# Elementwise work at the start of a fused RWKV-7 and attention block: from POOL to DVE and ACT, the low-rank 1-mu columns formed from results, the first weights on ACT's queue, a second shift buffer

## The chip, the cores and the metric

The kernel runs on one core of a Trainium2 chip. The metric is device time in microseconds (us), the median of several executions. The engines are PE (TensorE, matrix products), DVE (VectorE), ACT (ScalarE), POOL (GpSimd) and SP (SyncE, which here only issues DMAs). PEld is PE's weight load, which overlaps PE. Each engine works through its instructions in a fixed order; the DMA queues of SP and ACT feed the same 16 DMA engines.

## The reference, cut to what matters

```python
def reference(x, ...):                       # x: (1, 256, 2048), D = 2048, branches of 1024
    h = _rms_norm(x, pre_norm_g)             # x * rsqrt(mean(x^2) + eps) * g
    proj = h @ w_in                          # 2048 -> 8 * 1024 + 2 * 2048
    p_r, p_k, p_v, z_r, q_a, k_a, v_a, z_a, m_r, m_a = split(proj)
    # RWKV branch
    r = p_r + (_shift(p_r) - p_r) * mu_rkv[0]     # k and v alike; _shift moves by one token
    dh = _shift(h) - h
    xw = h + dh * mu_wa[0]
    xa = h + dh * mu_wa[1]
    w = exp(-DECAY_SCALE * sigmoid(w0 + tanh(xw @ w1) @ w2))     # low-rank: 2048 -> 64 -> 1024
    a = sigmoid(a0 + (xa @ a1) @ a2)
    y = group_norm(recurrence(r, w, k, v, kk, a)) + bonus
    y_r = y * silu(z_r)
    y_a = _chunk_band_attention(q_a, k_a, v_a, rel_bias) * silu(z_a)
    u_r, u_a = y_r @ w_branch_rwkv, y_a @ w_branch_attn
    merged = sigmoid(m_r + b0) * u_r + sigmoid(m_a + b1) * u_a
    return x + _rms_norm(merged @ w_out, post_norm_g)
```

## The kernel before

All matrix products run at float32 precision in two parts: each operand is split into an upper part `wh` rounded to float32r and a lower part `wl`, and a product of 128 rows of weights (a k-tile) is three matmuls. A group of weights is four k-tiles by 256 columns (512 KB). For every group SP issues a load into one of three buffers `raw`, ACT makes `wh` (L82, a copy of 128x1024) and DVE makes `wl` (L83, `raw` minus `wh`); that pair of steps is the helper `split`. PE then runs the group (L277), first a `wh`, then a `wl`, and so on.

The function `run_plan` plays the list `plan`: the products k0 and r0 (the first 256 columns of k and r) group by group in turn, then v0, `lora` (the first layer of both low-rank paths), k2, r2, v2, k4 and so on, with q, k, v and z of the attention between them, the merge gates mr and ma, the branch outputs ur and ua, and last the output product o. The weights' parts are made two groups ahead of their use; a scheduler then fixes each engine's order, so the instructions of an engine wait in one line.

The products k0, r0, v0, lora and k2 run before the norm's factor is known. They use `hr`, which is x times the norm's weights and lacks the factor per token; such a product has 16 k-tiles and 96 matmuls. The tiles `hr_A` (k-tiles 0 to 7), `hr_yrl` and `hr_yrh` are made by `first_raw` (ACT L146 the upper part, DVE L147 the lower) from the tiles `xT_UV` and `xT_R`, which `first_raw` also loads (L140), together with the weights of k0 (L141). `second_raw` loads the weights of r0 (L156) and sums x squared into `xs`. The norm's factor comes from `norm_factor`: two additions (L344, L345), a product with ones on PE (`rb`), a square root on ACT and a reciprocal on DVE (L349) into `rones`. `normalise` (L351 to L363) then multiplies x by the factor on POOL (L356) and makes the normalised operand `hn` on ACT (L359) and DVE (L360); r2 is its first user.

The low-rank product takes 256 columns: 64 of w1 and 64 of a1, times 1 - mu, and the same 128 columns times mu, whose result is shifted by a token and added. `lora_weights` loads the 128 columns into a staging tile `wa` and makes the four groups `lab` on POOL: two multiplications by mu (L397) and one subtraction (L398) a group. `lora_raw` splits a group; `lora_done` multiplies the result by the norm's factor (L368), adds the shifted half (L411, L412) and applies tanh (L413). `lw` (L444) is the second layer's product.

The tile with tag `xs` holds a product's result times the norm's factor, for the shift by one token (`xsk`, `xsr`, `xsv`, L368, then the shifted multiply-add at L727; `lsh` in `lora_done`; also z of `project_zr`, L781). It has one buffer. At the very start PE runs nine products of ones (L125, `wp`), which nothing reads.

Of the kernel before, what the change touches and what calls it, by code (L numbers as in the profile page):

```python
# [17 lines left out]
# units of side work fed in per group of four weight tiles: of the fronts (while and after r, k, v are made), and  # L18
# of the chains and the attention, every BD groups
# [4 lines left out]
# buffers of weight tiles: as loaded, upper parts, lower parts  # L24
# [3 lines left out]
# the pair of the RWKV gates that waits in a place of its own  # L28
ZI = 6
# products of ones at the start  # L30
NWARM = 9
# how the first group is cut: first tile, number of tiles
FIRST = ((0, 2), (2, 2))
# order of the products between r, k, v and the merge: q (q and k), z (gate) of attention, v (its values, by 512
# columns), r (gate of the RWKV branch), each with the first of its two pairs of heads
# [13 lines left out]
# columns of the packed per-channel vectors  # L49
# [7 lines left out]
# column blocks of w_in  # L57
# [5 lines left out]
def kernel(ctx: ExitStack, tc, x, xt, vecs, w_in, wa1, w2, a2, w0, rel, w_br, w_ba, w_out, post_g, out):  # L63
# [14 lines left out]
    def col(t, o):  # L78
        return t[:, o:o + 1]
# [8 lines left out]
    def w_load(src, k0, c0, nm):  # L88
        """Rows of 4 tiles, 256 columns."""
        t = w_tile(nm)  # L90
        nc.sync.dma_start(t, src[k0 * P:(k0 + 4) * P, c0:c0 + 256].rearrange("(k p) c -> p k c", p=P))
        return t

    def wide_chunks(src, c0, nm):
        """Rows of 2 tiles, 512 columns."""
# [10 lines left out]
    # ---- x, channel-major: first times the norm's weights only, for the products that run before the norm's  # L106
    # factor is known, then normalised; each in two float32r parts that lie side by side ----
# [11 lines left out]
    # the tensor engine's clock rises after a few microseconds of work: products of ones, which nothing reads,  # L119
    # while the first tiles are loaded  # L120
# [13 lines left out]
    def first_raw(g):  # L134
        def f(wh, wl):
            xg = xT[g // 2][:, (g % 2) * 4:(g % 2) * 4 + 4, :]
            raw = raw8[:, 2 * g]
            for k, n in FIRST if g == 0 else ((0, 4),):
                rows = slice((4 * g + k) * P, (4 * g + k + n) * P)
                nc.sync.dma_start(xg[:, k:k + n, :], xt[rows, :].rearrange("(k p) t -> p k t", p=P))  # L140
                nc.sync.dma_start(raw[:, k:k + n, :], w_in[rows, O_K:O_K + 256].rearrange("(k p) c -> p k c", p=P))  # L141
# [47 lines left out]
    # sums inside a chunk of 64, counted from its middle: of the tokens before token n, n = 0..64  # L189
# [9 lines left out]
    # masks of the chunk matrices: before the token (first half), up to the token (second half)  # L199
# [6 lines left out]
    # blocks of 16 below the diagonal, inside the diagonal blocks of 32  # L206
# [12 lines left out]
    # derived vectors: 1-mu for r, k, v; halves of k_a, a0, the merge biases  # L219
# [824 lines left out]
```

## Time and profile before

| what | value |
|---|---|
| device time, three executions | 878.86, 879.15, 877.31 us; median 878.86 us |
| profiled execution: span from first to last instruction | 877.4 us |
| profiled execution's own device time | not recorded apart from the span; the median of the three executions lies 1.5 us above the span |
| mean granted TensorE clock | 0.994 of full speed |
| PE busy | 854.3 us, 97% of the span |
| DVE busy | 592.7 us, 68% |
| ACT busy | 445.9 us, 51% |
| POOL busy | 46.2 us, 5% |

The span runs from the first to the last instruction of one profiled execution; the device time holds a little before and after it. Busy shares are averages over stages with different limits: POOL's 46.2 us, for instance, lie nearly all in the first 55 us.

### The profile page before, as it was taken

The numbers are of one execution on the slowest core, as the hardware profiler recorded it, in microseconds if no ns is written. First come the engines' busy times: TensorE is split into PE (matmuls) and PEld (weight loads), VectorE is DVE, ScalarE is ACT, GpSimd is POOL, SyncE is SP. The second block draws the span as 40 slices with busy tenths as digits, with TensorE's granted clock in tenths as the row PEclk, the third lists the DMA queues.
The fourth block names the chain that finished last, engine by engine and source line by source line (L and its number), as shares of the span: only waits on it lengthen the run. The fifth ranks groups of instructions, "written<-read, shape, count | busy, mean of one in ns | idle before, by whom it ended". The sixth has DMA issues, their size and how long they took to land.

```text
span 877.4 us, 14844 instructions
## 1 busy us (share of the span) xinstructions
PE 854.3 (97%) x5972; PEld 730.7 (83%) x5972; DVE 592.7 (68%) x826; ACT 445.9 (51%) x669; POOL 46.2 (5%) x82
## 2 busy tenths in 40 slices
PE   8979999999899999999999999999999999999996
PEld 7978888888787888888888888888888888888886
DVE  7998886966759866654976775565565565565554
ACT  7466564545455433444556664445444455444442
POOL 4840000000010000000000000000000000000000
PEclk9999999999999999999999999999999999999999
DMA  9706545664144555634475446666556656676662
GB/s 305 210 19 187 172 123 150 198 171 130 50 121 141 172 149 146 194 115 145 129 222 154 144 144 205 183 189 191 182 182 189 190 184 182 187 264 213 194 193 96
DMA packets 142791, 147.33 MB, mean 168 GB/s; under 512 B 13313, under 2 KB 131201, under 8 KB 142338
## 3 DMA queue, kind: packets, MB, share of 16 engines
q1 hardware_dynamic: 130178, 138.96, 51.8%
q10 hardware_dynamic: 12544, 7.42, 2.8%
q8 instruction: 47, 0.77, 0.4%
q14 instruction: 22, 0.18, 0.1%
HBM read 143.74 MB, written 2.62 MB: 167 GB/s over the span
## 4 chain that ended last, share of the span: by engine, by line
PE 89%; DVE 4%; DMA 3%; SPq 2%; issue 1%; ACT 0%; DVEq 0%; ACTq 0%
PE acc_mr L277 10%; PE acc_ma L277 10%; PE acc_o L277 9%; PE acc_q L277 5%; PE acc_ak L277 5%; PE acc_va L277 5%; PE acc_ur L277 5%; PE acc_ua L277 5%; PE acc_za L277 5%; PE acc_k L277 4%; PE acc_v L277 4%; PE acc_r L277 4%; PE acc_zr L277 3%; DMA raw_v<-w_in_d 2%; PE pA L545 1%; PE acc_lora L277 1%
## 5 line engine op out<-in xcount | busy, mean ns | idle before, releaser
L277 PE MATMUL acc_mr<-hn,wh_mr 128*128 128x512 f32 x256 | 91.3, 400 | 0.0
L277 PE MATMUL acc_ma<-hn,wh_ma 128*128 128x512 f32 x256 | 91.1, 399 | 0.0
L277 PE MATMUL acc_mr<-hn,wl_mr 128*128 128x256 f32 x256 | 72.1, 282 | 0.0
L277 PE MATMUL acc_ma<-hn,wl_ma 128*128 128x256 f32 x256 | 72.0, 281 | 0.0
L83 DVE TENSOR_TENSOR wl_mr<-raw_mr,wh_mr 128x1024 fp32r<-128x1024 f32 x32 | 39.2, 1225 | 34.2 <-ACT wh_mr L82 34.1
L83 DVE TENSOR_TENSOR wl_o<-raw_o,wh_o 128x1024 fp32r<-128x1024 f32 x31 | 38.0, 1225 | 34.0 <-ACT wh_o L82 33.9
L83 DVE TENSOR_TENSOR wl_ma<-raw_ma,wh_ma 128x1024 fp32r<-128x1024 f32 x32 | 39.2, 1225 | 29.4 <-ACT wh_ma L82 29.4
L277 PEld LDWEIGHTS acc_mr<-hn,wh_mr 128*128 128x128 f32 x256 | 48.1, 188 | 12.4 <-issue 0.7
L277 PEld LDWEIGHTS acc_ma<-hn,wh_ma 128*128 128x128 f32 x256 | 48.1, 188 | 12.3 <-issue 0.6
L82 ACT ACTIVATE wh_ma<-raw_ma 128x1024 fp32r<-128x1024 f32 x32 | 33.9, 1060 | 45.0 <-PE acc_mr L277 37.3
L82 ACT ACTIVATE wh_mr<-raw_mr 128x1024 fp32r<-128x1024 f32 x32 | 34.0, 1061 | 39.3 <-PE acc_ua L277 16.2
L82 ACT ACTIVATE wh_o<-raw_o 128x1024 fp32r<-128x1024 f32 x31 | 32.8, 1059 | 39.6 <-PE acc_o L277 24.8
L277 PE MATMUL acc_o<-wh_o,mgh 128*128 128x512 f32 (+1 forms) x140 | 49.8, 356 | 0.0
L277 PE MATMUL acc_o<-wl_o,mgh 128*128 128x512 f32 (+1 forms) x140 | 49.8, 356 | 0.0
L277 PEld LDWEIGHTS acc_mr<-hn,wl_mr 128*128 128x128 f32 x256 | 48.4, 189 | 0.1
L277 PEld LDWEIGHTS acc_ma<-hn,wl_ma 128*128 128x128 f32 x256 | 48.3, 189 | 0.0
L277 PE MATMUL acc_q<-hn,wh_q 128*128 128x512 f32 x128 | 45.9, 398 | 0.0
L277 PE MATMUL acc_zr<-hn,wh_zr 128*128 128x512 f32 x128 | 45.9, 400 | 0.0
L277 PE MATMUL acc_za<-hn,wh_za 128*128 128x512 f32 x128 | 45.8, 399 | 0.0
L277 PE MATMUL acc_ak<-hn,wh_ak 128*128 128x512 f32 x128 | 45.8, 397 | 0.0
L277 PE MATMUL acc_va<-wh_va,hn 128*128 128x512 f32 x128 | 41.0, 395 | 0.0
L277 PE MATMUL acc_ak<-hn,wl_ak 128*128 128x256 f32 x128 | 36.8, 288 | 0.0
(478 smaller groups left out, 2385.1 us busy)
## 6 DMA issues: line engine op xcount, KB each, us to landing
raw_mr<-w_in_d SPq DMA_DIRECT2D x32, 512.0 KB, 4.2
raw_ma<-w_in_d SPq DMA_DIRECT2D x32, 512.0 KB, 3.6
raw_o<-w_out_d SPq DMA_DIRECT2D x32, 512.0 KB, 4.4
raw_v<-w_in_d SPq DMA_DIRECT2D x16, 512.0 KB, 4.7
raw_q<-w_in_d SPq DMA_DIRECT2D x16, 512.0 KB, 4.4
raw_ak<-w_in_d SPq DMA_DIRECT2D x16, 512.0 KB, 3.6
raw_zr<-w_in_d SPq DMA_DIRECT2D x16, 512.0 KB, 3.7
raw_va<-w_in_d SPq DMA_DIRECT2D x16, 512.0 KB, 3.8
```

The source lines that it names most:

```text
L82: ACT.activation(h, src, AF.Copy)
L83: DVE.tensor_tensor(l, src, h.bitcast(F32), op=ALU.subtract)
L277: PE.matmul(d, u, v, start=first and n == 0, stop=last and n == len(ops) - 1)
L545: PE.matmul(pA[h][:, c * P:(c + 1) * P], AB[HS[h], m, c, 2:4, :].rearrange("p a t -> p (a t)"), AB[HS[h], m, c, 0:2, :].rearrange("p a t - ...
```

## The change

Five edits; the diff also takes out comments, so line numbers behind `normalise` are lower by some lines after it.

1. `first_raw` issues the two loads of k0's first weight group on ACT's queue; the three later groups stay on SP's.
2. `normalise` no longer uses POOL. DVE multiplies x by the norm's weight and factor in one instruction a k-tile (16 of 128x256), in place; then `split` makes the two parts in four instructions of 128x1024 on ACT and four on DVE. Before, POOL made four products of 128x1024, ACT 16 and DVE 16 instructions of 128x256.
3. `lora_weights` has no staging tile: four loads of 256 KB go straight into the left halves of `lab` (before, two of 512 KB into `wa`). The eight multiplications by mu move to DVE, 256 elements a partition each. The columns times 1 - mu are no longer made (four POOL subtractions of 128x512 go); the left half stays unscaled, and `lora_done` subtracts the mu half of the result from it, one DVE instruction of 128x256 more.
4. The tiles with tag `xs` (also `lsh` and z) get two buffers.
5. The program's dynamic DMA scratch size is set to 1024.

```diff
-                nc.sync.dma_start(raw[:, k:k + n, :], w_in[rows, O_K:O_K + 256].rearrange("(k p) c -> p k c", p=P))
+                (nc.sync if g else nc.scalar).dma_start(raw[:, k:k + n, :], w_in[rows, O_K:O_K + 256].rearrange("(k p) c -> p k c", p=P))
...
-            POOL.tensor_tensor(xg, xg, rbc.unsqueeze(1).to_broadcast([P, 4, T]), op=ALU.mult)
             for i in range(4):
-                pre = col(vt, V_PRE + 4 * g + i)
-                ACT.activation(hg[:, i, 0, :], xg[:, i, :], AF.Copy, scale=pre)
-                DVE.scalar_tensor_tensor(hg[:, i, 1, :], xg[:, i, :], pre, hg[:, i, 0, :].bitcast(F32), op0=ALU.mult, op1=ALU.subtract)
+                DVE.scalar_tensor_tensor(xg[:, i, :], xg[:, i, :], col(vt, V_PRE + 4 * g + i), rbc, op0=ALU.mult, op1=ALU.mult)
+            split(hg[:, :, 0, :], hg[:, :, 1, :], xg)
             yield
...
         if not q:
-            lab.append(bg.tile([P, 16, 128], F32, tag="AB0", name="wa"))
             ab = bg.tile([P, 8, 256], F32, tag="AB1", name="lab0")
...
-        wa = lab[0][:, 8 * q:8 * q + 8]
-        nc.sync.dma_start(wa, wa1[q * 1024:(q + 1) * 1024, :].rearrange("(k p) c -> p k c", p=P))
         for g in (2 * q, 2 * q + 1):
-            w = lab[0][:, 4 * g:4 * g + 4]
-            ab = lab[1 + g]
+            nc.sync.dma_start(lab[g][:, :, 0:128], wa1[g * 512:(g + 1) * 512, :].rearrange("(k p) c -> p k c", p=P))
+
+    def lora_raw(g):
+        def f(wh, wl):
+            ab = lab[g]
             for n, o in ((0, V_MUW), (1, V_MUA)):
                 mu = vt[:, o + 4 * g:o + 4 * g + 4].unsqueeze(2).to_broadcast([P, 4, 64])
-                POOL.tensor_tensor(ab[:, :, 128 + 64 * n:192 + 64 * n], w[:, :, 64 * n:64 * n + 64], mu, op=ALU.mult)
-            POOL.tensor_tensor(ab[:, :, 0:128], w, ab[:, :, 128:256], op=ALU.subtract)
-
-    def lora_raw(g):
-        def f(wh, wl):
-            split(wh, wl, lab[1 + g])
+                DVE.tensor_tensor(ab[:, :, 128 + 64 * n:192 + 64 * n], ab[:, :, 64 * n:64 * n + 64], mu, op=ALU.mult)
+            split(wh, wl, ab)
...
-        sh = tp.tile([P, 2, T + 1], F32, tag="xs", name="lsh", bufs=1)
+        sh = tp.tile([P, 2, T + 1], F32, tag="xs", name="lsh", bufs=2)
...
-        DVE.tensor_tensor(t[0:64], sh[0:64, 0, 1:T + 1], sh[0:64, 1, 0:T], op=ALU.add)
-        DVE.tensor_tensor(za[64:128], sh[64:128, 0, 1:T + 1], sh[64:128, 1, 0:T], op=ALU.add)
+        DVE.tensor_tensor(t, sh[:, 0, 1:T + 1], sh[:, 1, 1:T + 1], op=ALU.subtract)
+        DVE.tensor_tensor(t[0:64], t[0:64], sh[0:64, 1, 0:T], op=ALU.add)
+        DVE.tensor_tensor(za[64:128], t[64:128], sh[64:128, 1, 0:T], op=ALU.add)
```

On ACT's queue the start of the program reads so before (`vt` are the packed vectors, `warm` is a first use of the square root, `wh_k` and `wh_r` the upper parts of the first weights, `xs` the sum of squares):

```order
L117 ACTIVATE warm<-warm 128x1
L1000 ACTIVATE warm<-warm 128x1
L146 ACTIVATE hr_A<-xT_UV,vt 128x256 x2
L82 ACTIVATE wh_k_163<-raw_77 128x512
L146 ACTIVATE hr_A<-xT_UV,vt 128x256 x2
L160 ACTIVATE xs_83<-xT_UV 128x1024
L82 ACTIVATE wh_k_163<-raw_77 128x512
L82 ACTIVATE wh_r_181<-raw_77 128x1024
```

and so after the change:

```order
L117 ACTIVATE warm<-warm 128x1
L141 DMA raw_77<-w_in_d 128x2x256 x2
L146 ACTIVATE hr_A<-xT_UV,vt 128x256 x4
L160 ACTIVATE xs_83<-xT_UV 128x1024
L995 ACTIVATE warm<-warm 128x1
L82 ACTIVATE wh_k_163<-raw_77 128x512
L82 ACTIVATE wh_r_181<-raw_77 128x1024
L82 ACTIVATE wh_k_163<-raw_77 128x512
```

The two DMA issues are new there, and the first `wh_k` has moved behind all four `hr_A` and the squares.

On DVE, around the low-rank product, before (`wl_lora` are the lower parts of its four groups, `xsk`, `xsr` and `xsv` the results of k0, r0 and v0 times the norm's factor, `k` and `r` their shifted sums):

```order
L83 TENSOR_TENSOR wl_lora_569<-lab_306,wh_lora_568 128x1024
L727 SCALAR_TENSOR_TENSOR k_494<-xsk_491,vt,k_494 128x256 x2
L360 SCALAR_TENSOR_TENSOR hn<-xT_UV,vt,hn 128x256 x2
L368 TENSOR_TENSOR xsr_499<-acc_r_234,rones 128x2x256
L83 TENSOR_TENSOR wl_lora_597<-lab_306,wh_lora_596 128x1024
L360 SCALAR_TENSOR_TENSOR hn<-xT_UV,vt,hn 128x256 x6
L727 SCALAR_TENSOR_TENSOR r_502<-xsr_499,vt,r_502 128x256 x2
L83 TENSOR_TENSOR wl_lora_632<-lab_Y,wh_lora_631 128x1024
L360 SCALAR_TENSOR_TENSOR hn<-xT_R,vt,hn 128x256 x2
L368 TENSOR_TENSOR xsv_624<-acc_v_513,rones 128x2x256
L360 SCALAR_TENSOR_TENSOR hn<-xT_R,vt,hn 128x256 x2
L83 TENSOR_TENSOR wl_lora_671<-lab_s,wh_lora_670 128x1024
```

and after, from the second group of `lora` on (before it now stand `xsk`, `xsr` and twelve of the new multiplications at L357):

```order
L357 SCALAR_TENSOR_TENSOR xT_R<-xT_R,vt,rones 128x256 x4
L83 TENSOR_TENSOR wl_lora_588<-lab_305,wh_lora_587 128x1024
L722 SCALAR_TENSOR_TENSOR k_483<-xsk_480,vt,k_483 128x256 x2
L722 SCALAR_TENSOR_TENSOR r_491<-xsr_488,vt,r_491 128x256 x2
L357 SCALAR_TENSOR_TENSOR xT_R<-xT_R,vt,rones 128x256
L83 TENSOR_TENSOR wl_lora_625<-lab_Y,wh_lora_624 128x1024
L357 SCALAR_TENSOR_TENSOR xT_R<-xT_R,vt,rones 128x256 x2
L83 TENSOR_TENSOR hn<-xT_UV,hn 128x4x256
L357 SCALAR_TENSOR_TENSOR xT_R<-xT_R,vt,rones 128x256
L83 TENSOR_TENSOR hn<-xT_UV,hn 128x4x256
L83 TENSOR_TENSOR wl_lora_663<-lab_s,wh_lora_662 128x1024
```

Behind it the line goes on with `hn`, `xsv` and the first `wl_k` of k2.

The third place is DVE in front of that, from the third group of k0 to the first group of `lora`, after the change (the multiplications by mu, L395, are new; the `wl` and `xs` rows stood there before too):

```order
L395 TENSOR_TENSOR lab_305<-lab_305,vt 128x4x64 x2
L83 TENSOR_TENSOR wl_k_260<-raw_77,wh_k_259 128x1024
L395 TENSOR_TENSOR lab_305<-lab_305,vt 128x4x64 x2
L83 TENSOR_TENSOR wl_r_298<-raw_77,wh_r_297 128x1024
L147 SCALAR_TENSOR_TENSOR hr_yrh<-xT_R,vt,hr_yrh 128x256 x4
L164 TENSOR_TENSOR xs_83<-xs_83,xsq_375 128x1024
L395 TENSOR_TENSOR lab_Y<-lab_Y,vt 128x4x64
L83 TENSOR_TENSOR wl_k_333<-raw_77,wh_k_332 128x1024
L395 TENSOR_TENSOR lab_Y<-lab_Y,vt 128x4x64
L83 TENSOR_TENSOR wl_r_371<-raw_77,wh_r_370 128x1024
```

Then follow `xs` 128x512, two `wl_v`, `xs` 128x256, the last two multiplications by mu, two more `wl_v`, the reciprocal and the first `wl_lora`.

## Rows read from the trace of the kernel before

**Rows 1.** The page's busy times, and the shares of the chain that ended last by engine.

```profile
PE 854.3 (97%) x5972; PEld 730.7 (83%) x5972; DVE 592.7 (68%) x826; ACT 445.9 (51%) x669; POOL 46.2 (5%) x82
PE 89%; DVE 4%; DMA 3%; SPq 2%; issue 1%; ACT 0%; DVEq 0%; ACTq 0%
```

**Rows 2.** The waits of PE over the whole run: who waits, for whom, us in all, how many, the longest.

```profile
PE acc_lora L277 <- DVE wl_lora L83: 4.7, 1, 4.7
PE acc_k L277 <- DVE wl_k L83: 2.7, 3, 1.8
PE pw L643 <- DVE SB L682: 1.3, 1, 1.3
PE lw L444 <- issue: 1.3, 1, 1.3
```

**Rows 3.** Four stretches of the run: the stretch, its length, then busy us (and instructions) of PE, PEld, DVE, ACT, POOL, then the granted clock, the DMA engines' busy share and GB/s.

```profile
26.50:34.00 7.50, 5.67 (x48) 5.47 (x47) 7.50 (x6) 3.05 (x3) 7.50 (x6) 1.00 0.66 146
46.00:54.00 8.00, 3.33 (x28) 3.13 (x27) 8.00 (x7) 3.70 (x9) 5.64 (x4) 1.00 0.00 0
54.00:58.00 4.00, 3.94 (x20) 3.94 (x21) 4.00 (x10) 4.00 (x8) 1.09 (x2) 0.57 0.02 6
82.00:877.40 795.40, 783.15 (x5455) 663.69 (x5454) 518.37 (x732) 392.01 (x583) 7.25 (x20) 1.00 0.54 167
```

**Rows 4.** POOL in order of time: start, busy us, the instructions, and in brackets the idle time before them and what ended it.

```profile
19.51 4.45 POOL L397 TENSOR_TENSOR lab<-wa,vt 128x256 f32<-128x256 f32 x4 [12.06 <-DMA wa<-wa_d]
...
34.69 2.27 POOL L398 TENSOR_TENSOR lab_s<-wa,lab_s 128x512 f32<-128x512 f32 x1
39.78 6.77 POOL L356 TENSOR_TENSOR xT_UV<-xT_UV,rones 128x1024 f32<-128x1024 f32 x2 [2.82 <-DVE rones L349]
46.51 5.09 POOL L356 TENSOR_TENSOR xT_R<-xT_R,rones 128x1024 f32<-128x1024 f32 x2
```

**Rows 5.** DVE in order of time, columns as in rows 4.

```profile
13.88 1.22 DVE L83 TENSOR_TENSOR wl_k<-raw,wh_k 128x1024 fp32r<-128x1024 f32 x1
...
18.87 1.22 DVE L83 TENSOR_TENSOR wl_k<-raw,wh_k 128x1024 fp32r<-128x1024 f32 x1
20.00 1.22 DVE L83 TENSOR_TENSOR wl_r<-raw,wh_r 128x1024 fp32r<-128x1024 f32 x1
...
26.41 2.29 DVE L83 TENSOR_TENSOR wl_k<-raw,wh_k 128x1024 fp32r<-128x1024 f32 x1
...
31.19 0.83 DVE L345 TENSOR_TENSOR xs<-xs 128x256 f32<-128x256 f32 x1
...
37.96 1.74 DVE L349 RECIPROCAL rones<-rones 128x256 f32<-128x256 f32 x1
39.70 1.23 DVE L83 TENSOR_TENSOR wl_v<-raw_v,wh_v 128x1024 fp32r<-128x1024 f32 x1
40.84 0.69 DVE L368 TENSOR_TENSOR xsk<-acc_k,rones 128x512 f32<-128x512 f32 x1
41.44 2.83 DVE L83 TENSOR_TENSOR wl_lora<-lab,wh_lora 128x1024 fp32r<-128x1024 f32 x1
44.20 5.19 DVE L727 SCALAR_TENSOR_TENSOR k<-xsk,vt,k 128x256 f32<-128x256 f32 x2
...
52.80 1.21 DVE L83 TENSOR_TENSOR wl_lora<-lab,wh_lora 128x1024 fp32r<-128x1024 f32 x1
53.93 2.46 DVE L360 SCALAR_TENSOR_TENSOR hn<-xT_UV,vt,hn 128x256 fp32r<-128x256 f32 x6
```

**Rows 6.** PE in order of time, at the two longest waits and at `lw`.

```profile
28.75 0.38 PE L277 MATMUL acc_k<-hr_yrh,wl_k 128*128 128x256 f32 x1 [1.83 <-DVE wl_k L83]
...
46.05 0.40 PE L277 MATMUL acc_lora<-hr_A,wh_lora 128*128 128x256 f32 x2
...
54.06 0.43 PE L277 MATMUL acc_lora<-hr_A,wl_lora 128*128 128x256 f32 x1 [4.73 <-DVE wl_lora L83]
54.29 0.63 PE L277 MATMUL acc_lora<-hr_A,wh_lora 128*128 128x256 f32 x2
...
57.93 0.40 PE L277 MATMUL acc_lora<-hr_A,wh_lora 128*128 128x256 f32 x2
...
58.29 0.40 PE L277 MATMUL acc_lora<-hr_yrl,wh_lora 128*128 128x256 f32 x2
...
72.27 1.95 PE L444 MATMUL lw<-w2e,zw 65*128 65x512 f32 x4 [1.27 <-issue]
```

**Rows 7.** The start on PE, ACT and SP's queue, in order of time.

```profile
5.57 0.79 PE L277 MATMUL acc_k<-hr_A,wh_k 128*128 128x256 f32 x2 [0.21 <-ACT wh_k L82]
14.65 0.50 PE L277 MATMUL acc_r<-hr_A,wh_r 128*128 128x256 f32 x2 [0.45 <-ACT wh_r L82]
...
0.81 0.45 ACTq L109 DMA_DIRECT2D vt<-vecs_d  x1
...
4.09 0.91 ACT L146 ACTIVATE hr_A<-xT_UV,vt 128x256 fp32r<-128x256 f32 x2 [1.07 <-DMA xT_UV<-xt_d]
...
10.04 1.71 ACT L146 ACTIVATE hr_A<-xT_UV,vt 128x256 fp32r<-128x256 f32 x4 [0.35 <-DMA xT_UV<-xt_d]
...
4.44 1.33 SPq L156 DMA_DIRECT2D raw<-w_in_d  x1
```

**Rows 8.** The DMA issued by SP between 33 and 36 us: transfer, count, KB each, median us from issue to landing.

```profile
raw_v<-w_in_d SPq DMA_DIRECT2D x1, 512.0 KB, 4.9
```

More of the change, by code (lines that the diff above doesn't have):

```diff
@@ L715, in done @@
             nmk = "rkv"[what]
-            xs = tp.tile([P, 2, T + 1], F32, tag="xs", name=f"xs{nmk}{j0}", bufs=1)
+            xs = tp.tile([P, 2, T + 1], F32, tag="xs", name=f"xs{nmk}{j0}", bufs=2)
             POOL.memset(xs[:, :, 0:1], 0.0)
@@ L780, in done @@
                 yrt.extend(bg.tile([P, n, 2, T], F32R, tag=t, name=f"yr_{t}") for t, n in (("AB1", 4), ("w2", 2), ("s", 2)))
-            z = tp.tile([P, 2, T], F32, tag="iv" if j0 == ZI else "xs", name=f"zr{j0}", bufs=1)
+            z = tp.tile([P, 2, T], F32, tag="iv" if j0 == ZI else "xs", name=f"zr{j0}", bufs=1 if j0 == ZI else 2)
             z_gate(acc, f"r{j0}", z)
@@ L1033 @@
     }
-    nc = bacc.Bacc("TRN2", target_bir_lowering=False, num_devices=1)
+    nc = bacc.Bacc("TRN2", target_bir_lowering=False, num_devices=1, dynamic_dma_scratch_size=1024)
     args, ins = [], {}
```

## The prediction

> **What bounds the kernel now.** I read the busy times first, then the chain, then PE's waits, and then the stretches in which PE waits. PE is busy in 97% of the span and holds 89% of the chain that ended last [rows 1], so time can only be won where PE idles or runs at a lower clock. Over the whole run its largest waits are 4.7 us in `lora` for a `wl_lora` of DVE, 2.7 us in three pieces for a `wl_k` of DVE, and 1.3 us before `lw` [rows 2]. After 82 us PE is busy 783.15 of 795.40 us and no wait that the list names is over 1.3 us [rows 2, 3]: the change must win its time before that.
>
> Two places carry the waits. At 28.75 us PE has waited 1.83 us for the last group of k0, and at 54.06 us 4.73 us for the second group of `lora` [rows 6]. In both stretches DVE and POOL are at work together: DVE is busy 7.50 of 7.50 us and 8.00 of 8.00, POOL 7.50 and 5.64 [rows 3]. The same instruction of DVE, a 128x1024 subtraction, took 1.22 us at 18.87 and at 20.00 us, before POOL began at 19.51 or just as it did, but 2.29 us at 26.41 and 2.83 us at 41.44 [rows 5], with POOL at work. POOL's first block ended at 34.69 + 2.27 = 36.96 us and its second began at 39.78 [rows 4]; in that gap the 1024 subtraction took 1.23 us again, at 39.70 us. Two shifted sums of 128x256 took 5.19 us at 44.20 us, 2.6 each; six instructions of that kind took 2.46 at 53.93, 0.41 each, when POOL had ended at 51.60 [rows 4, 5]. So DVE is slowed two to six times by POOL, and the late `wl` are what PE waits for.
>
> The Trainium skill, page "SBUF — State Buffer", section "SBUF: two separate sides", says why that may be: a DVE instruction with two SBUF operands and a GpSimd instruction that reads SBUF take one pair of ports in turn, and the one that comes later blocks until the other has ended. The traced 2.29 and 2.83 us against 1.22 agree with it. The sum below would be the same without the page.
>
> **The change part by part.** Prices of DVE alone, start to start: 128x1024 1.13 us (18.87 to 20.00), 128x512 0.60 (40.84 to 41.44), 128x256 0.41 (2.46/6), the reciprocal 1.74 [rows 5].
>
> *What it gives.* With no POOL arithmetic, the wait of 1.83 us at 28.75 goes if DVE gets there in time, and the 4.73 us at 54.06 [rows 6]. Behind the latter the clock was low: in 54 to 58 us the granted clock was 0.57 [rows 3], nearer the 1.2 than the 2.4 GHz level. From 54.29 to 57.93 us six k-tile halves (a `wh` pair and a `wl`) took 3.64 us, while one at full clock takes 58.29 - 57.93 = 0.36 [rows 6]; 3.64 - 6 x 0.36 = 1.5 us, which go with the wait that brought them. The wait of 1.27 us before `lw` [rows 6] goes too: in the new order `lw` stands behind k2, not in its third group, so it no longer comes as soon as `lora_done` allows. Nothing shows that wait's cause ("issue"), so its bounds are 0 and 1.3; I take 1.3, since the new place is some 3 us later. Sum: 1.8 + 4.7 + 1.5 + 1.3 = 9.3 us.
>
> *What DVE now has to do.* It gains eight multiplications by mu, sixteen multiplications of x and four subtractions of 1024, and loses sixteen of 128x256. The question is when each `wl_lora` is ready. A walk in the new order: `wl_r` of the third group began at 20.00 us [rows 5]; four multiplications by mu now stand ahead of it, 4 x 0.41 = 1.6, and 0.4 is allowed for the wait on their loads, which landed by 19.51 [rows 4]: 22.0. To it are added `wl_r` 1.13, four `hr` 1.64, `xs` 1.13, mu 0.4, `wl_k` 1.13, mu 0.4, `wl_r` 1.13, `xs` 0.6: 29.6. The `wl_k` of the last group is ready at 27.8, against 28.75 before; PE first needs it at 28.75 - 1.83 = 26.9, plus a later start of 0.3 (below) 27.2, so 0.6 of the 1.8 could stay, and the two `wl_k` waits of rows 2 beside the longest (0.9 in all) may go: I set these against each other. Two `wl_v` 2.3, `xs` 0.4, two mu 0.8, `wl_v` 1.13 give 34.2. The fourth `wl_v` waits for its load, issued when the first buffer is free (about 30.7 in the walk), 4.9 us to landing [rows 8] and about a microsecond on ACT: some 37.4 when done. Reciprocal 1.74, `wl_lora` 1.13, `xsk` and `xsr` 1.2, twelve multiplications 4.9, `wl_lora` 1.13: 47.5. Four `k` and `r` and one multiplication 2.05, `wl_lora` 1.13: 50.7. Then three multiplications 1.2, two `hn` of 1024 2.3 and the last `wl_lora` 1.13: 55.3.
>
> *When PE needs them.* `lora` began at 46.05 [rows 6]; less 1.8 and plus the start's 0.3 it is 44.55. A group of eight halves of 0.36 is 2.88, so the groups are due at 44.55, 47.4, 50.3 and 53.2. The first three are ready in time or within 0.4; the last comes 2.1 late less what the third took: in all 1.9 to 2.1 of wait, I take 1.9. Bounds: 0, if the fourth `wl_v` lands 2 us earlier, and 5, if the mu multiplications cost as the contended 0.83 (31.19 us) [rows 5], 8 x 0.42 = 3.4 more. A wait of 1.83 us left the clock at full (1.00 in 26.5 to 34) [rows 3, 6], so I add no clock loss to it. k2's first `wl` is due behind `lora` at 57.9; three more instructions (1024, 512, 1024) put it at 58.2: no further wait.
>
> *The first weights.* ACT now issues two DMAs ahead of the first `hr_A` and makes all four `hr_A` and the squares before the first `wh_k`. An issue took ACT 0.45 us at 0.81 us, SP 1.33 at 4.44 us [rows 7]. Ending at about 3.7 the two cheap ones lie ahead of the 4.09 at which x landed [rows 7]. Four `hr_A` 1.7, squares and warm 1.2 and `wh_k` 0.6 put PE's first product at 7.6 instead of 5.57 [rows 7]. What covers it: the second group's x came for ACT at 10.04 and its `wl_k` began at 13.88, ready at 15.1; PE had caught up with them, as its wait of 0.45 at 14.65 says [rows 5, 7]. The first group's 32 halves are 5.8 us, 7.6 + 5.8 = 13.4, so about 1.7 us of slack takes the delay, and 0.3 is left for `wl` that come late in it. Without that cover: 1.5 for the clock that falls if PE idles from 5.4 (5.57 less its wait of 0.21) to 7.6 (as after 54 us), and 1.4 if the issues take ACT 1.33 each (5.45 instead of 4.09): together with the 0.3, 3.2 us. Bounds 0 and 3.2, value 0.3.
>
> *The rest.* Two loads of 512 KB become four of 256 KB on SP's queue, and two go from there to ACT's: as many issues on SP as before. One more subtraction in `lora_done` (0.41) and the second shift buffer I cost at nothing: behind `lora` PE has k2, 11.5 us (32 halves of 0.36), to cover them. ACT loses 16 instructions and gains four. The scratch size does nothing that the trace shows.
>
> **Sum.** 877.4 - 9.3 + 1.9 + 0.3 = 870.3 us of span; the median lies 878.86 - 877.4 = 1.5 above the span, so I forecast 871.8.
>
> **The rivals.**
>
> *The start costs its full 3.2 us* (clock or issues, as above): 871.8 + 2.9 = 874.7. For it: PE idles about 2 us more at the start than before. Against: the 1.83 us wait did not drop the clock [rows 3, 6]. The Trainium skill, "TensorE: Matmul & The Clock Gate", section "Part 1: The HAM clock gate", says that an idle TensorE goes to half rate and needs work to come back; in this trace 4.73 us of idling did that and 1.83 did not.
>
> *The mu multiplications are dear*, 0.83 each: their operands are a stride of 64 columns and a repeated column, which no DVE row before shows; 871.8 + 3.4 = 875.2.
>
> *DVE's slowness is not POOL's doing* and stays; then DVE has only been given more work, and the kernel is slower. Ahead of the last `wl_lora` it has 8 + 16 new 128x256 and two new 1024 less twelve old 128x256; at the contended 0.83 and 2.29, 12 x 0.83 + 2 x 2.29 = 14.5 us. `lora`'s end moves by that, less 1.3 at `lw`: 878.9 + 13.2 = 892.1. It decides as soon as the walk from 22.0 to 55.3 takes 7.2 us, 22%, longer than at the prices alone. For it: DVE was also full there, so a common cause (PE's or ACT's traffic) is thinkable. Against: 1.23 and 0.69 us in POOL's gap, with PE and ACT as busy as around it.
>
> *Nothing changes*: an earlier start of r2 is given back later, to weights that do not come earlier: 878.9. For it: the DMA engines are 54% busy all along [rows 3]. Against: after 82 us PE's waits are small, and the loads are issued when buffers come free, not at fixed times.
>
> **How the numbers follow.** My forecast has 0.60, the dear start 0.18, the dear multiplications 0.06, the slow DVE 0.08, nothing changed 0.08. The forecast's own range is 868.7 (no wait in `lora`, no start cost, and the 0.9 of small `wl_k` waits gone) to 874.1 (`lw`'s wait stays, and another microsecond in `lora`). The range of 8 in 10 takes in the dear start and the dear multiplications: 868.5 to 876.0. A measurement of this kernel tells about 0.2% (1.8 us) from no change. Faster: 0.60 + 0.18 + 0.06 = 0.84; same 0.08; slower 0.08.
>
> **What would show it.** Right: every 128x1024 on DVE between 20 and 55 us takes 1.2 us; no PE wait at `wl_k` of the last group over 1 us; one of about 2 us at the last `wl_lora` instead of 4.7 at the second; a clock of 1.00 in 54 to 58 us; r2 some 7 us before its old start; PE's idle time after that unchanged. Wrong: 1024 subtractions of 2 us with POOL idle; a low clock between 6 and 13 us; a first product after 9 us; a new wait of PE behind k2 or in the chunk chains.

## The result, and the profile after

The changed kernel takes 871.35 us (median of four executions, 869.36 to 873.26) against 878.48 us before: a ratio of 0.9922, 95% interval 0.9906 to 0.9937. Timed again later it took 870.89 us, ratio 0.9921 (0.9908 to 0.9935). The forecast was 871.8. The profiled execution took 871.44 us, with a span of 869.7 us.

The page's busy times and the chain's shares, which answer to [rows 1]:

```profile
PE 852.2 (98%) x5972; PEld 729.3 (84%) x5972; DVE 585.3 (67%) x839; ACT 444.4 (51%) x657; POOL 16.6 (2%) x66
PE 92%; DMA 3%; DVE 2%; SPq 2%; issue 1%; ACT 1%; DVEq 0%; ACTq 0%
```

DVE has 2% of the chain instead of 4%, and although it has 13 instructions more it is busy 7 us less. (The share alone says little: `e_warm` below, with the same time, has 4%.) PE's waits (us in all, how many, the longest) answer to [rows 2]:

```profile
PE acc_k L277 <- ACT wh_k L82: 2.9, 1, 2.9
PE lw L439 <- issue: 1.7, 1, 1.7
...
PE acc_v L277 <- ACT wh_v L82: 1.0, 1, 1.0
```

No wait for a `wl` is left in the list. The largest wait is the start. The stretches, with the columns of [rows 3]:

```profile
7.00:12.00 5.00, 4.21 (x22) 3.99 (x23) 3.90 (x8) 4.83 (x11) 0.18 (x2) 0.66 1.09 349
...
26.50:34.00 7.50, 6.46 (x54) 6.26 (x53) 6.87 (x10) 3.17 (x3) 0.00 (x0) 1.00 0.83 222
...
46.00:54.00 8.00, 8.00 (x69) 8.00 (x68) 8.00 (x13) 5.72 (x7) 0.76 (x3) 1.00 0.01 2
54.00:58.00 4.00, 4.00 (x35) 3.97 (x34) 4.00 (x5) 1.97 (x3) 1.35 (x2) 1.00 0.00 0
...
70.00:82.00 12.00, 11.44 (x48) 8.63 (x49) 10.26 (x14) 10.65 (x19) 0.10 (x1) 0.86 0.43 134
```

From 46 to 58 us PE is busy throughout at full clock, where before it was busy 3.33 of 8.00 and then at 0.57. But from 7 to 12 us the clock is 0.66 and from 70 to 82 us it is 0.86, and in the first profile of before both were 1.00. DVE and PE in order of time, as in [rows 5, 6, 7]:

```profile
18.44 0.76 DVE L395 TENSOR_TENSOR lab<-lab,vt 128x256 f32<-128x256 f32 x2
...
40.84 3.26 DVE L357 SCALAR_TENSOR_TENSOR xT_UV<-xT_UV,vt,rones 128x256 f32<-128x256 f32 x8
...
53.30 1.23 DVE L83 TENSOR_TENSOR wl_lora<-lab_s,wh_lora 128x1024 fp32r<-128x1024 f32 x1
```

```profile
7.79 0.80 PE L277 MATMUL acc_k<-hr_A,wh_k 128*128 128x256 f32 x2 [2.94 <-ACT wh_k L82]
...
28.40 0.51 PE L277 MATMUL acc_v<-hr_A,wh_v 128*128 128x256 f32 x2 [1.04 <-ACT wh_v L82]
...
70.56 1.96 PE L439 MATMUL lw<-w2e,zw 65*128 65x512 f32 x4 [1.70 <-issue]
```

Every 128x1024 subtraction takes 1.2 us, a multiplication of x 0.41 where eight follow each other (3.26/8), one by mu 0.38 in a pair (0.76/2): near the prices of the sum. A single one shows up to 0.49. The first column of the table below says where PE is; the starts and ends are those of its matmuls in the trace.

| place | before | after | difference | second profile of each, difference |
|---|---|---|---|---|
| `lora` starts | 46.05 | 45.72 | -0.3 | 48.84, 45.67: -3.2 |
| `lora` ends | 64.58 | 57.47 | -7.1 | 65.69, 57.40: -8.3 |
| k6 starts | 152.35 | 147.48 | -4.9 | 153.24, 149.02: -4.2 |
| last za of the front pairs starts | 343.75 | 338.64 | -5.1 | 344.62, 340.35: -4.3 |
| next q starts | 365.92 | 358.04 | -7.9 | 364.74, 360.08: -4.7 |
| span | 877.4 | 869.7 | -7.7 | 876.2, 871.8: -4.4 |

So in the first pair 6.8 us are won inside `lora` and 2.2 are lost again by k6; in the second 5.1 are won there and 4.1 lost. The 2.8 that the first pair wins between 339 and 366 us are for the larger part not there in the second. From the next q to the end it is 511.5 to 511.7 us in all four profiles. The second profile of after is of the execution of 873.59 us, the longest of its five (the others 869.98 to 872.25). The first of before should be that of 879.15 us, the longest of its four: that is an estimate from the other profiles, where the time is 1.7 us above the span. The two profiles nearest to the medians are the first of after (871.44) and the second of before (877.95); between these the differences are -3.1, -8.2, -5.8, -6.0, -6.7 and -6.5 us.

### The profile page after: what moved, and what is told of

Its sections match the earlier page's. It is cut to its first block, busy times and chain, and to the rows that moved or that the text cites. A ratio compares the mean times of both kernels' runs of the same rounds, so it can differ in the third digit from the quotient of the medians.

```text
span 869.7 us, 14822 instructions
## 1 busy us (share of the span) xinstructions
PE 852.2 (98%) x5972; PEld 729.3 (84%) x5972; DVE 585.3 (67%) x839; ACT 444.4 (51%) x657; POOL 16.6 (2%) x66
## 4 chain that ended last, share of the span: by engine, by line
PE 92%; DMA 3%; DVE 2%; SPq 2%; issue 1%; ACT 1%; DVEq 0%; ACTq 0%
PE acc_mr L277 10%; PE acc_ma L277 10%; PE acc_o L277 9%; PE acc_ak L277 5%; PE acc_zr L277 5%; PE acc_za L277 5%; PE acc_va L277 5%; PE acc_ur L277 5%; PE acc_ua L277 5%; PE acc_q L277 5%; PE acc_k L277 4%; PE acc_r L277 4%; PE acc_v L277 4%; PE acc_lora L277 1%; PE pA L540 1%; DMA raw_v<-w_in_d 1%
## 5 line engine op out<-in xcount | busy, mean ns | idle before, releaser
L277 PE MATMUL acc_q<-hn,wl_q 128*128 128x256 f32 x128 | 36.8, 288 | 0.0
```

The costliest lines, as they stand in the source:

```text
L277: PE.matmul(d, u, v, start=first and n == 0, stop=last and n == len(ops) - 1)
```

## The experiments

Each number is a median of several executions, with the ratio to the kernel before on the same chip and its 95% interval. All are to be held against the changed kernel's 871.35 and 870.89, ratios 0.9922 and 0.9921.

**First weights back on SP's queue (e_sp).**

```diff
-                (nc.sync if g else nc.scalar).dma_start(raw[:, k:k + n, :], ...)
+                nc.sync.dma_start(raw[:, k:k + n, :], ...)
```

> The changed kernel with edit 1 undone: the first group's weights of k0 go back to SP's queue. Theory A (read from the two traces): PE's first product comes at 5.6 us instead of 7.8 and the low clock from 7.8 to 10.8 goes, some 1.5 us of PE time, but the last wl_lora of DVE, which now comes just in time (it ended at 54.5 us, PE needed it at 54.4), then makes PE wait 1 to 1.5 us: the time stays at 871.3 within 0.6. Theory B (the start is paid in full): 2.2 of later start and 1.4 of low clock come back, 868 us, with no new wait in lora. Theory C (the prediction's start cost of 0.3): 871.0, and a wait of under 0.5 in lora.

871.30 us, 0.9932 (0.9913 to 0.9952): no difference in the median. The spread is wider: four of the twelve executions took 874.61 to 877.01 us, while all nine of the changed kernel lie between 869.36 and 873.59. The profiled execution took 870.33 us, so what made those four long stays open. In it PE's first product comes at 5.81 us and the clock is full from 7 to 12 us, but `lora` starts at 45.40 instead of 45.72. The waits of PE say where the 2 us went:

```profile
PE acc_v L277 <- ACT wh_v L82: 1.0, 1, 1.0
...
PE acc_r L277 <- ACT wh_r L82: 0.4, 1, 0.4
```

PE waits for upper parts of ACT, 0.45 us at 14.86 and 0.96 at 28.09 us. The second are v0's first weights, which ACT began at 26.98 us instead of 27.29 although PE had started 2 us earlier. Theory A's time holds, but its place is wrong: no wait in `lora`. Theory C fits: the prediction's 0.3 for the start is what the trace shows.

**More products of ones at the start (e_warm).**

```diff
-NWARM = 9
+NWARM = 16
```

> The changed kernel with 16 instead of 9 products of ones at the start, so that PE does not idle before its first product at 7.8 us. Theory A (PE's start is covered: k0 and r0 end when the loads allow it): the clock is full from 7.8 us on, the time in front of v0's first wh grows by as much, lora starts within 0.4 us of 45.7, 871.3 within 0.7. Theory B (the low clock at the start is paid): lora starts 1.4 us earlier, 870.

870.67 us, 0.9920 (0.9908 to 0.9933): theory A. The clock is 1.00 from 7 to 12 us, and the wait in front of v0 has grown by 0.7:

```profile
28.72 0.51 PE L277 MATMUL acc_v<-hr_A,wh_v 128*128 128x256 f32 x2 [1.70 <-ACT wh_v L82]
```

`lora` starts at 46.04.

**Normalisation back on POOL (e_norm_pool).**

```diff
-                DVE.scalar_tensor_tensor(xg[:, i, :], xg[:, i, :], col(vt, V_PRE + 4 * g + i), rbc, ...)
-            split(hg[:, :, 0, :], hg[:, :, 1, :], xg)
+            POOL.tensor_tensor(xg, xg, rbc.unsqueeze(1).to_broadcast([P, 4, T]), op=ALU.mult)
             for i in range(4):
+                pre = col(vt, V_PRE + 4 * g + i)
+                ACT.activation(hg[:, i, 0, :], xg[:, i, :], AF.Copy, scale=pre)
+                DVE.scalar_tensor_tensor(hg[:, i, 1, :], xg[:, i, :], pre, hg[:, i, 0, :].bitcast(F32), op0=ALU.mult, op1=ALU.subtract)
```

> The changed kernel with edit 2 undone: the four 128x1024 products of the normalisation are back on POOL (from about 38.6 us on, where the norm's factor is ready), with the sixteen small instructions on ACT and DVE. Theory A (POOL's arithmetic slows DVE): 128x1024 subtractions of DVE take 1.2 us before 38 us and 2.3 to 2.8 between 39 and 51 us, PE waits 3 to 6 us for wl_lora and the time is 875 to 878. Theory B (the slowness has another cause): DVE has less to do and is no slower, lora does not wait, 871 us or less.

877.33 us, 0.9988 (0.9977 to 0.9999): nearly all of the gain is gone. The profiled execution took 874.46 us, the lowest of twelve, so the rows show some 3 us of the 6 that the median loses. POOL, then DVE, in order of time, then PE's wait, then the stretch behind it:

```profile
38.84 6.62 POOL L356 TENSOR_TENSOR xT_UV<-xT_UV,rones 128x1024 f32<-128x1024 f32 x2 [31.75 <-DVE rones L349]
```

```profile
33.34 1.22 DVE L83 TENSOR_TENSOR wl_v<-raw_v,wh_v 128x1024 fp32r<-128x1024 f32 x1
...
43.12 5.18 DVE L724 SCALAR_TENSOR_TENSOR k<-xsk,vt,k 128x256 f32<-128x256 f32 x2
...
54.49 1.66 DVE L360 SCALAR_TENSOR_TENSOR hn<-xT_UV,vt,hn 128x256 fp32r<-128x256 f32 x4
```

```profile
PE acc_lora L277 <- DVE wl_lora L83: 2.0, 1, 2.0
```

```profile
54.00:58.00 4.00, 3.98 (x21) 3.98 (x22) 4.00 (x9) 3.40 (x8) 1.68 (x2) 0.58 0.00 0
```

DVE is slow while POOL multiplies, 2.6 us for a shifted sum (0.44 in the changed kernel, at 46.73), and quick before and after it (1.22 for a 128x1024 at 33.34, 0.41 for a 128x256 at 54.49): that the slowness is POOL's doing is shown, and the rival that it has another cause falls. PE's wait is 2.0 us where theory A expected 3 to 6.

**The whole low-rank preparation back on POOL (e_lora_pool):** staging tile, multiplications by mu, the subtraction for 1 - mu, and one sum less behind the product.

```diff
+            lab.append(bg.tile([P, 16, 128], F32, tag="AB0", name="wa"))
...
+                POOL.tensor_tensor(ab[:, :, 128 + 64 * n:192 + 64 * n], w[:, :, 64 * n:64 * n + 64], mu, op=ALU.mult)
+            POOL.tensor_tensor(ab[:, :, 0:128], w, ab[:, :, 128:256], op=ALU.subtract)
...
-                DVE.tensor_tensor(ab[:, :, 128 + 64 * n:192 + 64 * n], ab[:, :, 64 * n:64 * n + 64], mu, op=ALU.mult)
...
-        DVE.tensor_tensor(t, sh[:, 0, 1:T + 1], sh[:, 1, 1:T + 1], op=ALU.subtract)
...
```

> The changed kernel with edit 3 undone as a whole: staging tile, both multiplications by mu and the subtraction for 1 - mu on POOL again, one sum less after the product. Theory A (edit 3 gains by what it leaves out, POOL's four 128x512 subtractions and so 9 us of slowed DVE, not by moving the multiplications, which alone changed nothing): DVE is slowed from 19.5 to 37 us, the last wl_k of k0 is late (PE waits 1.8 to 2.5 us near 28 to 30 us), 872.5 to 874. Theory B (only the normalisation on POOL mattered, since it meets lora): the same as the changed kernel within 0.7.

875.35 us, 0.9970 (0.9958 to 0.9982): theory A's mechanism, and dearer than it expected (the profiled execution took 873.96 us). DVE in order of time and PE's waits:

```profile
26.46 2.31 DVE L83 TENSOR_TENSOR wl_k<-raw,wh_k 128x1024 fp32r<-128x1024 f32 x1
...
32.02 6.09 DVE L83 TENSOR_TENSOR wl_v<-raw_v,wh_v 128x1024 fp32r<-128x1024 f32 x3
```

```profile
PE acc_lora L277 <- DVE wl_lora L83: 3.1, 1, 3.1
...
PE acc_k L277 <- DVE wl_k L83: 1.2, 2, 1.0
```

The wait at `wl_k` that theory A named is 1.0 us; the larger one, in `lora`, it did not name. POOL ended at 37.0 us, and still `lora` waits 3.1 us at 52.5: the late `wl_v` push the whole line of DVE back.

**Only the multiplications by mu back on POOL (e_mu_pool).**

```diff
-                DVE.tensor_tensor(ab[:, :, 128 + 64 * n:192 + 64 * n], ...)
+                POOL.tensor_tensor(ab[:, :, 128 + 64 * n:192 + 64 * n], ...)
```

> The changed kernel with the eight multiplications by mu back on POOL; the columns times 1 - mu stay away. Theory A (POOL's reads slow DVE): DVE's 128x1024 subtractions take 2 us or more from about 19.5 to 31 us and 1.2 after it; the last wl_k of k0 is late as before the change (PE waits 1 to 2 us near 28 us), lora does not wait, 872 to 873.5. Theory B (the multiplications are cheaper on POOL, and DVE gets through earlier): no longer subtractions, 870 to 871.

870.56 us, 0.9923 (0.9905 to 0.9941): the same, which is theory B's time. Theory A's 128x1024 subtractions of 2 us do not come (they take 1.21 to 1.63), but other rows of DVE are slowed. POOL now runs in pieces:

```profile
18.14 5.56 POOL L395 TENSOR_TENSOR lab<-lab,vt 128x256 f32<-128x256 f32 x4 [10.95 <-DMA lab<-wa_d]
25.36 2.39 POOL L395 TENSOR_TENSOR lab_Y<-lab_Y,vt 128x256 f32<-128x256 f32 x2 [1.65 <-DMA lab_Y<-wa_d]
```

```profile
20.96 3.03 DVE L147 SCALAR_TENSOR_TENSOR hr_yrh<-xT_R,vt,hr_yrh 128x256 fp32r<-128x256 f32 x4
...
25.04 1.21 DVE L83 TENSOR_TENSOR wl_k<-raw,wh_k 128x1024 fp32r<-128x1024 f32 x1
```

DVE's 128x1024 subtractions took 1.22 us at 18.61 and 19.75, with POOL at work since 18.14; there it was POOL's first multiplication that took long, 3.30 us where later ones took 0.79. Then four `hr` took 3.03 instead of 1.67. What DVE loses by it it gains by not multiplying. Where the multiplications run is worth nothing here; by difference the 4 us that e_lora_pool loses belong to the rest of edit 3, of which POOL's four 128x512 subtractions (8.2 us of POOL) are the largest part. That is argued, not shown: they were not tried apart from the staging tile, nor without the multiplications beside them.

**One shift buffer (e_xs1).**

```diff
-        sh = tp.tile([P, 2, T + 1], F32, tag="xs", name="lsh", bufs=2)
+        sh = tp.tile([P, 2, T + 1], F32, tag="xs", name="lsh", bufs=1)
...
-            xs = tp.tile([P, 2, T + 1], F32, tag="xs", name=f"xs{nmk}{j0}", bufs=2)
+            xs = tp.tile([P, 2, T + 1], F32, tag="xs", name=f"xs{nmk}{j0}", bufs=1)
...
```

> The changed kernel with edit 4 undone: tiles with tag xs (the shifted results and z) have one buffer again. Theory A (the second buffer is what shortened the stretch from 318 to 360 us by 2.8 us): the waits z<-T 1.2 and xx<-issue 1.1 are back near 350 us, and the time is 874 us or more. Theory B (that stretch differed for another reason, edit 4 is worth nothing): 871.3 within 0.6, and those waits are absent, or they come and go between profiles whatever the buffers. In its instruction order lw stands earlier in k2 than in the changed kernel, so under either theory up to 1.5 us more at lw.

877.99 us, 0.9994 (0.9981 to 1.0007): the whole gain is gone, and at a place that neither theory named.

```profile
PE acc_k L277 <- DVE xsv L366: 5.7, 1, 5.7
```

```profile
53.98 0.68 DVE L366 TENSOR_TENSOR xsr<-acc_r,rones 128x512 f32<-128x512 f32 x1
...
59.12 0.87 DVE L722 SCALAR_TENSOR_TENSOR r<-xsr,vt,r 128x256 f32<-128x256 f32 x2
60.87 1.23 DVE L83 TENSOR_TENSOR wl_k<-raw_k,wh_k 128x1024 fp32r<-128x1024 f32 x1 [0.88 <-ACT wh_k L82]
62.01 0.69 DVE L366 TENSOR_TENSOR xsv<-acc_v,rones 128x512 f32<-128x512 f32 x1
```

```profile
58.00:62.00 4.00, 0.00 (x0) 0.00 (x0) 3.12 (x5) 1.06 (x1) 0.11 (x1) 0.80 0.83 248
62.00:66.00 4.00, 3.16 (x15) 3.19 (x16) 3.15 (x8) 2.75 (x5) 0.10 (x1) 0.50 0.85 270
```

The results of v0, `lora` and k2 share two accumulators, so k2 can start only when `xsv` has read v0's. `xsv` needs the shift buffer, which `xsr` holds until r's two sums at 59.12 us, and those stand behind `wl_k` and `hn` in DVE's line; `xsv` itself then stands behind one more `wl_k`. `lora` is through at 57.2; PE waits 5.65 us and then runs at half clock. The smaller scratch of edit 5 is still in this run, so the loss is not its doing. In the kernel before, the same `xsv` came at 59.02 us and cost nothing, because `lora`'s own stall held PE until 61.4:

```profile
59.02 0.68 DVE L368 TENSOR_TENSOR xsv<-acc_v,rones 128x512 f32<-128x512 f32 x1
```

```profile
61.41 0.40 PE L277 MATMUL acc_k<-hr_A,wh_k 128*128 128x256 f32 x2
```

(The waits near 350 us do not decide theory A either: 0.7 us of `xx` here.)

**Two shift buffers in the kernel before, alone (b_xs2).** The smaller DMA scratch of edit 5 comes with it.

```diff
-            xs = tp.tile([P, 2, T + 1], F32, tag="xs", name=f"xs{nmk}{j0}", bufs=1)
+            xs = tp.tile([P, 2, T + 1], F32, tag="xs", name=f"xs{nmk}{j0}", bufs=2)
...
-    nc = bacc.Bacc("TRN2", target_bir_lowering=False, num_devices=1)
+    nc = bacc.Bacc("TRN2", target_bir_lowering=False, num_devices=1, dynamic_dma_scratch_size=1024)
```

> The kernel before with edit 4 alone (two buffers for the tiles with tag xs; edit 5, the smaller scratch, comes with it because the second buffer needs its room). Theory A (the buffer's wait is hidden behind the stall in lora, which DVE and POOL make and which stays): PE's wait of 4.7 us for wl_lora is there, and the time is 877 to 879. Theory B (the one buffer is what cost the time, whatever POOL does): 872 us.

879.82 us, 1.0021 (1.0010 to 1.0033): theory A's mechanism, with a time a shade above its 877 to 879. PE's waits show the stalls that stay, the one in `lora` at 2.9 us:

```profile
PE acc_k L277 <- DVE wl_k L83: 3.0, 4, 1.8
PE acc_lora L277 <- DVE wl_lora L83: 2.9, 1, 2.9
```

**`lw` later (e_lw8):** in `lora_end`, eight empty steps go ahead of `group_decay(0)` in the queue that is fed in between the groups.

```diff
         side.insert(0, group_decay(0))
+        side.insert(0, (None for _ in range(8)))
```

> The changed kernel with the second low-rank layer (lw) fed in four groups later, in the middle of r2. Theory A (lw is an early customer of the low-rank result, and PE's 1.7 us wait in front of it with the low clock from 72.3 to 75.6 us behind it cost 3 us): the wait and the low clock are gone, 868 us. Theory B (PE would wait for the weights or hn of r2 there anyway): another wait of 1 us or more between 66 and 76 us, and 871 us.

871.54 us, 0.9919 (0.9904 to 0.9933): no difference, but not for theory B's reason. Wait and low clock are gone (1.00 from 66 to 78 us) and r2 starts 3.6 us earlier, at 69.31. The RWKV chain, which was fed in later with it, takes that back at 211 to 225 us:

```profile
PE pg L664 <- DVE UV L652: 2.3, 2, 1.7
PE acc_zr L277 <- DVE aq L369: 1.4, 1, 1.4
```

**The sums behind the low-rank product on POOL (e_lzpool):** the three instructions of `lora_done` that make `lz` and `za` go from DVE to POOL, and tanh is written ahead of the last.

```diff
-        DVE.tensor_tensor(t, sh[:, 0, 1:T + 1], sh[:, 1, 1:T + 1], op=ALU.subtract)
-        DVE.tensor_tensor(t[0:64], t[0:64], sh[0:64, 1, 0:T], op=ALU.add)
-        DVE.tensor_tensor(za[64:128], t[64:128], sh[64:128, 1, 0:T], op=ALU.add)
+        POOL.tensor_tensor(t, sh[:, 0, 1:T + 1], sh[:, 1, 1:T + 1], op=ALU.subtract)
+        POOL.tensor_tensor(t[0:64], t[0:64], sh[0:64, 1, 0:T], op=ALU.add)
         ACT.activation(zw[0:64, :], t[0:64], AF.Tanh)
+        POOL.tensor_tensor(za[64:128], t[64:128], sh[64:128, 1, 0:T], op=ALU.add)
```

> The changed kernel with the three sums that follow the low-rank product (in lora_done) on POOL, which is idle there; in ACT's order the tanh then stands ahead of the second upper part of r2 instead of behind it. Theory A (on DVE and ACT these short steps stand behind parts of r2's weights that wait for their loads, and this makes lw late by 1.7 us with a low clock of 1.5 us behind it): no wait before lw, no low clock from 72 to 76 us, r2 some 3 us earlier; 868.5 us if nothing gives it back, 871 if the later chain of the RWKV branch does. Theory B (POOL's slower sums and its hold on DVE cost as much): the wait at lw stays at 1 us or more, 871 to 872.

869.93 us, 0.9904 (0.9885 to 0.9923): the lowest time of the study, but its interval overlaps that of the changed kernel. The profiled execution took 872.28 us, the longest of four, with v0's first weights late (a wait of 1.8 us at 30.24), and shows a wait of 1.62 us at `lw`:

```profile
70.12 1.28 ACT L407 ACT_TABLE_LOAD   x1
71.42 0.42 ACT L407 ACTIVATE zw<-lz 64x256 f32<-64x256 f32 x1
```

`lz` was ready at 67.58, but tanh still stands behind a `wh_r` that waited 2.94 us for its load, and behind the load of ACT's function table (1.28 us). So the wait is there as theory B said, though not for its reason, POOL's slower sums; and the time alone does not settle it.

**Both small moves to POOL together (e_mulz):** the edits of e_mu_pool and e_lzpool.

> The changed kernel with both small moves that were each as fast or faster: the multiplications by mu and the three sums after the low-rank product on POOL; only the normalisation and the missing 1 - mu columns remain of the move away from POOL. Theory A (the two are independent: mu's DVE time is spare before 38 us, the sums make lw earlier): 869 to 870. Theory B (each was within the spread and nothing more): 871 to 871.5.

872.61 us, 0.9938 (0.9920 to 0.9957), with single executions from 870.06 to 875.55: nothing is added up, and neither theory's time is met. No version beats the changed kernel by more than the spread.

**The two kernels again (b_again, a_again),** with nothing edited.

> The kernel before, unchanged, profiled once more. In the first pair of profiles 2.8 us of the gain lie between 318 and 360 us, where PE waits for T (1.2 us) and xx (1.1 us) in the kernel before and not after the change. Theory A (that stretch differs because of the change): the two waits are there again, with the same starts of the products within 0.3 us. Theory B (it is a difference between executions): they are shorter or gone, and the span is 875 to 877.

> The changed kernel, unchanged, profiled and timed once more, since the first profile of it and of the kernel before differ in places that the change doesn't touch. Theory A (PE's start at v0, the wait before lw and the clock behind it move by about 1 us each between executions, since they hang on loads): first product near 7.8 us, no wait over 0.5 us in lora, r2 from 72 to 74 us, but the low clock behind lw there or not; 870.5 to 872.5. Theory B (all places repeat): the same waits within 0.2 us, among them 1.0 at 28.4, 1.7 at lw with the low clock behind it.

In the second profile of before (877.95 us, one execution) the wait for T is gone, that for `xx` is 0.2 us, and its stretch from za to q is 20.1 us instead of 22.2 (after: 19.4 and 19.7): theory B, most of the late 2.8 us differs between executions and is not the change's. The two large stalls are there again, in other sizes:

```profile
PE acc_k L277 <- DVE wl_k L83: 3.4, 2, 2.5
PE acc_lora L277 <- DVE wl_lora L83: 3.1, 1, 3.1
```

In the second profile of after the wait before v0 is 0.5 instead of 1.0, `lora` has none again, `lw` waits 1.64 us, and the low clock behind it is longer: the wait at `lw` repeats, as theory B said, and the two others move, as theory A said.

```profile
70.00:74.00 4.00, 3.55 (x6) 1.71 (x7) 2.34 (x3) 3.08 (x5) 0.00 (x0) 0.62 0.59 178
74.00:78.00 4.00, 4.00 (x14) 3.40 (x13) 2.95 (x5) 2.74 (x5) 0.10 (x1) 0.53 0.50 148
```

## Why the prediction was right, and where it was not

The time came out right, 871.35 for 871.8, and its main cause was the right one; but the sum was right by terms that missed in both directions, and that they cancel to half a microsecond is luck. Up to k6 the sum has a gain of 7.1 us; the profiles show 4.9 and 4.2 there, and 5.8 between the two nearest to the medians.

*POOL slows DVE, and the late `wl` stall PE* (right). The runs with POOL's work put back show it: 877.33 and 875.35 us, with the slow rows of DVE only where POOL reads. The price of DVE's new work, 0.41 for a 128x256, was 0.38 to 0.41 in rows of several. The rivals of dear multiplications and of a slowness that is not POOL's fall. One reading behind it does not hold: the 1.23 us at 39.70 and the 0.69 at 40.84 are not in POOL's gap, as POOL had begun again at 39.78 [rows 4, 5]. The rows that show DVE quick with POOL idle are the one at 18.87 and, after 51.60, those at 52.80 and 53.93.

*4.7 + 1.5 us in `lora`* (right for the first profile of before; its second has a wait of 3.1). PE runs through at full clock. *The new wait of 1.9 at the last `wl_lora`* (wrong): there is none. The walk gave 55.3 us; it ended at 53.30 + 1.23 = 54.5, since the reciprocal came at 36.90 and not at 37.4. And PE needed it at 45.72 + 3 x 2.88 = 54.4, later than the 53.2 of the walk, because `lora` had not started earlier.

*1.8 us at 28.75* (its size stays open). The wait for `wl_k` went, and a wait of 1.04 for v0's first `wh` came, from none (e_mu_pool, e_xs1) to 1.8 (e_lzpool) in the other profiles: behind the late `wl_k` lay late loads. `lora` starts 0.3 us earlier in the first pair and 3.2 in the second, where 1.5 were expected; the kernel before itself differs by 2.8 there. In the walk to that `wl_k` the terms add up to 27.4 us and not to 27.8; the trace has 25.83 + 1.22 = 27.05.

*The start, 0.3 of 0 to 3.2* (right): its product comes 2.2 us later and at low clock, which the prediction had among its signs of being wrong; but e_sp, which takes both away, and e_warm, which takes the low clock away, gain nothing in the median. (The first group of k0 and r0 is 16 halves, not 32; its 5.8 us are right.)

*`lw`, a gain of 1.3* (wrong sign). The new place is no later in time, 70.56 us against 72.27: `lora` itself ends 7 us earlier, and `zw` does not keep up. The trace has the links, DVE first, then ACT:

```profile
65.90 1.23 DVE L83 TENSOR_TENSOR wl_r<-raw_r,wh_r 128x1024 fp32r<-128x1024 f32 x1 [1.90 <-ACT wh_r L82]
67.04 0.41 DVE L406 TENSOR_TENSOR lz<-lz,lsh 64x256 f32<-64x256 f32 x1
```

```profile
67.67 1.06 ACT L82 ACTIVATE wh_r<-raw_r 128x1024 fp32r<-128x1024 f32 x1 [1.29 <-DMA raw_r<-w_in_d]
68.75 1.28 ACT L408 ACT_TABLE_LOAD   x1
70.05 0.42 ACT L408 ACTIVATE zw<-lz 64x256 f32<-64x256 f32 x1
```

The second sum of `lz` stands behind a `wl_r`, tanh behind a `wh_r`, and both wait for r2's loads. In front of tanh ACT also loads its function table, 1.28 us, and does so only when the `wh_r` is through, though `lz` was ready at 67.45. From these rows the `wh_r` and the table load cost tanh some 1.3 us each (an estimate; no run takes the table load away. In e_xs1 it ran at 64.18, before `lz` was there, and `lw` had no wait). PE waits 1.70 us, and then the clock falls from 72 to 75.5 us (0.56 there): about 3 us lost where 1.3 were counted as won. The step that failed is the one that read the cause of "issue" as the place of `lw` in PE's order. The trace of the kernel before had the cause: `lz` was ready at 68.53 us, and tanh stood behind a `wh_k` that waited for its load, a 128x512 and the same table load:

```profile
70.46 1.28 ACT L413 ACT_TABLE_LOAD   x1
71.76 0.42 ACT L413 ACTIVATE zw<-lz 64x256 f32<-64x256 f32 x1
```

*The second shift buffer, costed at nothing* (wrong). It is worth all of the gain, 6.6 us: 877.99 without it. The cover that the prediction named, k2's own 11.5 us, is the product that waits. The sum came out right only because the edit was in the change, and so with its wait already gone. In the kernel before, the buffer's wait lay under `lora`'s stall, so no row of it showed; that an accumulator of k2 hangs on `xsv` could have been read from the code, as the walk had `xsv` behind the last `wl_lora` in any case.

*After 82 us nothing changes* (right within what two profiles tell): from k6 to the last za the difference stays at 4.9 to 5.1 us (4.2 to 4.3 in the second pair), and from the next q to the end all four profiles take the same.

The three edits that count are not additive, by the medians: without the normalisation on DVE 6.0 us are lost of the 7.1, without the low-rank edit 4.0, without the buffer 6.6; and the buffer alone in the kernel before wins nothing.

## What to carry to other kernels

When a stall is taken away, walk PE's next product through everything that it needs, its accumulator too, and ask which of these the old stall was covering: here a one-buffer tile behind it would have taken the whole gain. An edit that is worth nothing alone may be what lets another one pay, so undo each edit from the whole as well as trying each by itself. And short steps that a product waits for (sums, tanh) should not stand in an engine's line behind work that waits for a load; nor need the table load of such a step wait until its input is there.

## What the hardware showed that I had not expected

- The clock's falls do not follow from the length of PE's wait alone. It fell to 0.50 to 0.62 after waits of 1.04 (e_mulz, 73 to 75 us), 1.44 (e_norm_pool), 1.64 and 1.70 us before `lw`, and after the 2.04 us in `lora` of e_norm_pool (0.58); it stayed at 1.00 after 1.83 us [rows 3, 6], after 1.70 in front of v0 (e_warm) and after 1.62 before `lw` (e_lzpool). What decides it the runs do not tell. Nor does the mean clock order the times of the changed kernel: of its nine executions the two at 0.993 took 869.36 and 871.44 us, the one at 0.994 took 873.26, and the longest, 873.59, had 0.989.
- POOL's memsets do not slow DVE: while two of 64x1024 ran on POOL at 53.45 to 55.4 us after the change, DVE's 128x1024 at 53.30 and the next one took 1.23 us each. POOL's multiplications and subtractions, which read, made it up to 2.83. That fits the rule of the Trainium skill, page "SBUF — State Buffer", section "SBUF: two separate sides", which for DVE instructions with two SBUF inputs names only GpSimd instructions that read SBUF.
- It is not always DVE that is slowed. When POOL began beside a busy DVE, at 19.51 us in the kernel before and at 18.14 in e_mu_pool, DVE's 128x1024 subtractions went on at 1.22 us, and POOL's first multiplication took 2.19 and 3.30 us, where the later ones of that block took 0.79. After it DVE was slowed.
